# Transposes ahead of their copies, single first blocks on two queues, and short products at unit starts, in one layer of a hybrid decoder

## The chip, the cores and the metric

The kernel runs on one core of one Trainium2 chip. The metric is the device time of one execution in microseconds (us), and the figure to predict is the median over runs. Engines are named as the profile names them: PE is the matrix engine, PEld its weight load, DVE the vector engine, ACT the scalar engine, POOL the general engine, and SP the engine that issues most transfers. "SPq" and "ACTq" are the issue queues of SP and ACT.

## The reference, cut to what matters

One layer works on `x` of 256 tokens by 1024 channels, in float32.

```
h    = RMSNorm(x)
proj = h @ w_in                    # 1024 x 5656: queries, keys, values, gates, merge logits
o_a  = nsa_attention(...)          # compressed, selected and window attention, 8 heads
o_b  = dilated_attention(...)      # 3 groups of 4 heads
mixed = sigmoid(g_a) * (o_a @ w_proj_nsa) + sigmoid(g_b) * (o_b @ w_proj_dil)
x    = x + mixed @ w_out           # 1024 x 1024
h    = RMSNorm(x)
u, gate = split(h @ w_up)          # 1024 x 5632
x    = x + (gelu(conv(u)) * gate) @ w_down     # conv: causal, per channel, width 3; 2816 x 1024
out  = RMSNorm_final(x)
```

## The kernel before

**Work in units.** The host cuts all weights into units of at most 128 x 2240 numbers, in the order of their use, and the loop at the end of the program runs over them. Units 0 to 2 are the first columns of `w_in`; 3 to 15 are its queries, keys and values with the two hidden layers of the compression; 16 to 23 the merge logits; 24 to 26 the two mixer projections (unit 24 is the first half of `w_proj_nsa`); 27 to 30 `w_out`. Unit 31 (`NFIRST`) is the first unit of the feed-forward part: there follow pairs of up units (the `u` half and the gate half of 256 of the 2816 channels), and from the third pair on a down unit behind each pair. A down unit works on what a pair two pairs earlier gave (`LAG = 2`). There are eleven pairs and eleven down units; the last two downs are taken up in a closing part (`last`) of another order.

**One product in three.** All numbers are float32. Each operand is split into a rounded high part and the low rest, and a product is high x high, high x low and low x high. For a weight unit SP loads `raw`, ACT copies it into the high part `whi` (L128, called in `hi_of`, two units ahead), and DVE subtracts that into the low part `wlo` (L132, `lo_of`, one unit ahead). `raw`, `whi` and `wlo` have three buffers each. `parts` then issues on PE first all products with the high weight (L175), then all with the low weight (L180), which need DVE's part. A full unit has 48 products of 256 columns, 32 at L175 and 16 at L180, each with a weight load of its own.

**The short product.** When `rt["kick"]` is set, `parts` issues at its start one product more, of 64 columns (L170), with the operands of the unit's first product. It writes into the first 64 columns of the unit's own accumulator, which the product behind it starts afresh. Before, it is set for one unit, 33 (the third up unit).

**Accumulators.** There are eight banks: tags `d`, `o` and `t` with two tiles of one bank each, and `s` with one tile of two banks. Up pairs alternate between `d` and `o`. The down units add into four banks (`s` and both `t`) over all eleven of them.

**The residual.** The sum `x` after the mixers is held with channels on partitions, as `xT`. The down sums have tokens on partitions, so after unit 32 sixteen transposes (L1150) bring `xT` into four banks and ACT copies each bank into `X` (L1151). These lines are

```
ps2 = pd([2, 512], "s")
for q in range(4):
    t, h = q // 2, q % 2
    p = pd([512], "t") if t == 0 else ps2[:, h]
    for c in range(4):
        T.transpose(p[:, c * 128:c * 128 + 128], xT[:, 4 * h + c, t * 128:(t + 1) * 128], ident)
    A.activation(X[:, t, h * 512:(h + 1) * 512], p, AF.Copy)
```

**The start.** `x` and the weights of units 0 and 1 come together, in five blocks `first` over the eight k tiles of 128 channels (`CHUNKS` says how many k tiles each has). The first block goes out in two halves of 64 partitions, one from SP and one from ACT; all others, then unit 2, `xn`, `small` and the later units go out from SP (`load_to` keeps five units ahead). For each block ACT and DVE split `x` (`split_x`, L199 and L200) and the two weights (L1054 and L1055). Two products of 512 columns on a constant (L1027; the profile shows each as two) run ahead of the first block.

The order on each engine is the order of the code; no scheduler moves anything.

Of the kernel before, what the change touches and what calls it, by code (L numbers as in the profile page):

```python
# [14 lines left out]
AF = mybir.ActivationFunctionType  # L15
# [6 lines left out]
NF = DFF // 256  # L22
DIN = 5656
LAG = 2
CHUNKS = (1, 1, 2, 2, 2)
SHARED = {25: 1024, 26: 1024}
EPS = 1e-6
BIG = 1e30
# [47 lines left out]
def first_units(w):  # L76
# [3 lines left out]
    k0, out = 0, []  # L80
    for n in CHUNKS:
        c = f[:, k0:k0 + n].reshape(128, -1)
# [11 lines left out]
def build(ctx, tc, a, out):  # L94
    nc = tc.nc
    V, A, P, T = nc.vector, nc.scalar, nc.gpsimd, nc.tensor
# [7 lines left out]
    def pd(shape, tag="d"):  # L104
        return ps.tile([128] + shape, F32, name="ps_" + tag, tag=tag, bufs=1 if tag == "s" else 2)

    xT = const.tile([128, 8, S], F32, name="xT")
# [3 lines left out]
    ident = const.tile([128, 128], F32, name="ident")  # L111
# [5 lines left out]
    nhalf, inv_d, epsc = cst[:, 0:2], cst[:, 2:3], cst[:, 3:4]  # L117
# [44 lines left out]
    def parts(groups, w_stationary=True, start=True, stop=True):  # L162


        banks = set()
        if rt.pop("kick", False):

            (wh, _, xh, _), po = groups[0][2][0], groups[0][1]
            l, r = (wh, xh) if w_stationary else (xh, wh)
            T.matmul(po[:, :64], l, r[:, :64], start=True, stop=True, skip_group_check=True)  # L170
        for (bank, po, ks) in groups:
            for (wh, wl, xh, xl) in ks:
                for x in (xh, xl):
                    l, r = (wh, x) if w_stationary else (x, wh)
                    T.matmul(po, l, r, start=start and bank not in banks, stop=False, skip_group_check=True)  # L175
                    banks.add(bank)
        for (bank, po, ks) in groups:
            for n, (wh, wl, xh, xl) in enumerate(ks):
                l, r = (wl, xh) if w_stationary else (xh, wl)
                T.matmul(po, l, r, start=False, stop=stop and n == len(ks) - 1, skip_group_check=True)  # L180

    def w3(u, k):
        n = u.n // k
        return (u.hi[:, u.o:u.o + u.n].rearrange("p (k c) -> p k c", k=k),
                u.lo[:, u.o:u.o + u.n].rearrange("p (k c) -> p k c", k=k))
# [40 lines left out]
    def bc(R, n):  # L226
# [14 lines left out]
    scB = att.tile([128, 16], F32, name="scB")  # L241

    first = [att.tile([128, n * 768 + 8 * (t == "QS")], F32, name="first", tag=t)
             for n, t in zip(CHUNKS, ("QS", "MA", "qb", "kb", "vb"))]
    M = {}

    def mixer_tiles():
# [7 lines left out]
    rt = {}  # L255
# [74 lines left out]
    def mm_first(u):  # L330
# [15 lines left out]
        k0, late = 0, None  # L346
        for n in CHUNKS:
            for v in range(2):
# [264 lines left out]
    def mm_down_part(u, j, tcs, c0=0, c1=512, own=None):  # L613
        wh, wl = w3(u, 2)
        h, l = ffn["a", j]
        parts([((t, ch), ffn["y"][t][ch][:, b:e] if own is None else own,
                [(wh[:, kt, ch * 512 + b:ch * 512 + e], wl[:, kt, ch * 512 + b:ch * 512 + e],
                  h[:, kt, t * 128:t * 128 + 128], l[:, kt, t * 128:t * 128 + 128]) for kt in range(2)])
               for (t, ch) in tcs for b, e in ([(0, 256), (256, 512)] if c1 - c0 == 512 else [(c0, c1)])],
              False, start=j == (0 if own is None else NF - 2), stop=j == NF - 1)  # L620

    def mm_down(j):
        def f(u):
            if j == 0:
                s2 = pd([2, 512], "s")
                ta = pd([512], "t")
                tb = pd([512], "t")
                ffn["y"] = [[s2[:, 0], s2[:, 1]], [ta, tb]]
            if j < NF - 2:
                mm_down_part(u, j, [(t, ch) for t in range(2) for ch in range(2)])  # L630
        return f

# [13 lines left out]
    NFIRST = len(units)  # L646
# [7 lines left out]
    off = -2 * 128 * 2048  # L654
# [344 lines left out]
    u0, u1 = units[0], units[1]  # L999
# [9 lines left out]
    k0 = off = 0  # L1009
    for n, f in zip(CHUNKS, first):  # L1010
        w = f.shape[-1]
        for q, lo, hi in ((nc.sync, 0, 128),) if k0 else ((nc.sync, 0, 64), (nc.scalar, 64, 128)):
            q.dma_start(f[lo:hi], bass.AP(tensor=a["first"].tensor, offset=a["first"].offset + off + lo * w,
                                          ap=[[w, hi - lo], [1, w]]))
        k0 += n
        off += 128 * w
    u2 = units[2]
# [5 lines left out]
    nc.sync.dma_start(sm_, a["small"])  # L1023
    A.activation(tiny[:, 15:16], epsc, AF.Exp)
    pw = pd([512], "t")
    for _ in range(2):
        T.matmul(pw, epsc.to_broadcast([128, 128]), epsc.to_broadcast([128, 512]), start=True, stop=True)  # L1027
    kc0 = att.tile([128, 32], F32, name="kc0")
    V.memset(kc0, 0.0)
    cmp_["kc"] = kc0  # L1030
# [13 lines left out]
    k0 = 0  # L1044
    for n in CHUNKS:
        f = tiles.pop(0)
        f = f[:, 0:n * 768].rearrange("p (k c) -> p k c", k=n)
        for kt in range(k0, k0 + n):
            split_x(kt, f[:, kt - k0, 0:256], first[0][:, 768:776])
        for v, u in enumerate((u0, u1)):  # L1050
            r = f[:, :, 256 + 256 * v:512 + 256 * v]
            h, h32, l = [q[:, k0 * 256:(k0 + n) * 256].rearrange("p (k c) -> p k c", c=256)
                         for q in (u.hi, u.hi.bitcast(F32), u.lo)]
            A.activation(h, r, AF.Copy)  # L1054
            V.tensor_sub(l, r, h32)  # L1055
        k0 += n

# [17 lines left out]
    def at(i):  # L1075
        return items.get(i, [])

    post = []
    for i, u in enumerate(units):
        load_to(i + LA)  # L1080
        for it in at(i - 3):
            it.fin()
        for it in at(i - 2):
            it.te()
        for it in at(i - 1):
            it.sm()
        if i == 10:
            cmp_gelu()
        if i == 2:
            hi_of(3)  # L1090
            lo_of(3)
        if i == 9:
            for it in at(i - 1):
                it.sm2()
        if i > 2:
            lo_of(i + 1)
        if i != 9:
            for it in at(i - 1):
                it.sm2()
        if i == 14:  # L1100
            nc.sync.dma_start(xT, a["xT"])
        if i == 3:
            hi_of(5)
            mixer_tiles()
            u1.evac(u1)
            xc_tile()
            split_cmp(0)
            split_cmp(1)
        if i == 5:
            q_parts(0)  # L1110
            gates_of()
        if i == 6:
            q_parts(1)
        if i == 9:
            cmp_sum()
        if i == 11:
            cmp_kv_ev()
        if i == 14:

            ob = att.tile([128, 4, S], F32R, name="ob", tag="qa")  # L1120
            OB.update(h=ob[:, 0:2], l=ob[:, 2:4])
        if i in (23, 24):
            m = ML[i - 23]
            A.activation(m, m, AF.Sigmoid)
        if i == NFIRST:
            st.close()
            ffn["pool"] = ctx.enter_context(tc.tile_pool(name="ffn", bufs=1))
            gf = ffn["pool"].tile([128, D], F32, name="gf")
            nc.scalar.dma_start(gf, bass.AP(tensor=a["g_final"].tensor, offset=a["g_final"].offset,
                                            ap=[[0, 128], [1, D]]))  # L1130
            X = ffn["pool"].tile([128, 2, D], F32, name="X")
            sq = ffn["pool"].tile([128, 512], F32, name="sq")
        if 24 <= i <= 25:
            hi_of(i + 2)
        if i == NFIRST + 2:
            rt["kick"] = True
        u.mm(u)
        if not 24 <= i <= 26 and i > 1 and i != 3:
            hi_of(i + 2)
        if i == 2:  # L1140
            u0.evac(u0)
        if i == NFIRST + 1:
            rt["R2"] = rows_of(rt["rs2"], "R2", "o")
            units[NFIRST].evac(units[NFIRST])
            ps2 = pd([2, 512], "s")
            for q in range(4):
                t, h = q // 2, q % 2
                p = pd([512], "t") if t == 0 else ps2[:, h]
                for c in range(4):
                    T.transpose(p[:, c * 128:c * 128 + 128], xT[:, 4 * h + c, t * 128:(t + 1) * 128], ident)  # L1150
                A.activation(X[:, t, h * 512:(h + 1) * 512], p, AF.Copy)  # L1151
        if post:
            post.pop()()
        if u.pre:
            u.pre(u)
        if u.evac and i not in (0, 1, NFIRST):
            u.evac(u)
        if u.pre:
            post.append(post_g(len([q for q in units[:i] if q.pre])))
        for it in at(i - 2):  # L1160
            it.pv()
        for it in at(i - 1):
            it.tr()
        for it in at(i):
            it.qk()
        if i == 9:
            cmp_fold()
        if i == 10:
            cmp_kv()
# [63 lines left out]
```

## Time and profile before

| | |
|---|---|
| median of 3 runs | 415.38 us (415.17 to 415.42) |
| the profiled execution, its own time | 412.21 us |
| its span | 410.4 us |
| PE busy | 395.7 us, 96% of the span |
| PEld busy | 384.2 us, 94% |
| DVE busy | 290.6 us, 71% |
| ACT busy | 212.3 us, 52% |
| granted clock of PE, mean over the span | 0.997 |
| read from memory | 71.02 MB, 176 GB/s over the span |

The span runs from the first to the last recorded instruction; the execution's own time has in addition what lies around it. Busy shares are over the whole span, while products on PE overlap one another, so a busy PE is not yet a PE at its quickest. Starts and lengths in rows are us from the start of the span.

### The profile page before, as it was taken

To read this page: it belongs to the slowest core of one execution; us is meant where nothing else is said; L and a number is where in the kernel's file an instruction comes from. 1 tells how busy PE (TensorE), PEld (TensorE's weight loads), DVE (VectorE), ACT (ScalarE), POOL (GpSimd) and SP (SyncE) were. 2 spreads that over 40 slices of the span, in tenths; PEclk is the share of its full clock that TensorE was granted. 3 is DMA by queue.
4 is the path that set the end of the run, shared out by engine and by line. 5 is a ranking of instruction groups with operands and counts; after the bars stand their busy time and mean duration, and the time that the engine had idled before them with its cause. 6 is when DMAs were issued, how large, how long until landed. Compare 5 with 4: busy or idle time off the path is not lost.

```text
span 410.4 us, 8001 instructions
## 1 busy us (share of the span) xinstructions
PE 395.7 (96%) x3409; PEld 384.2 (94%) x3409; DVE 290.6 (71%) x483; ACT 212.3 (52%) x292; POOL 30.7 (7%) x58
## 2 busy tenths in 40 slices
PE   6999999999999999999999799999999999999993
PEld 3999989999998989999999799999999999999992
DVE  3988987887786657468797399494584865946753
ACT  4868563456664345663554766264254552653512
POOL 7010000000000000061143000000000000000012
PEclk9999999999999999999999999999999999999998
DMA  8963755235422532452556336743835627347002
GB/s 272 422 251 119 286 212 206 104 117 232 166 104 102 193 118 104 137 178 101 216 191 238 122 118 232 266 149 160 303 107 207 216 105 296 131 177 277 33 0 102
DMA packets 10851, 72.57 MB, mean 177 GB/s; under 512 B 1216, under 2 KB 1472, under 8 KB 2752
## 3 DMA queue, kind: packets, MB, share of 16 engines
q1 hardware_dynamic: 10448, 71.15, 47.4%
q10 hardware_dynamic: 368, 0.92, 0.7%
q8 instruction: 26, 0.43, 0.4%
q14 instruction: 9, 0.07, 0.1%
HBM read 71.02 MB, written 1.05 MB: 176 GB/s over the span
## 4 chain that ended last, share of the span: by engine, by line
PE 82%; DVE 6%; DMA 6%; ACT 3%; issue 2%; SPq 0%; POOLq 0%; POOL 0%; ACTq 0%
PE ps_d L175 24%; PE ps_o L175 12%; PE ps_d L180 12%; PE ps_o L180 6%; PE ps_s L175 5%; DMA raw<-in_wts_dram 5%; PE ps_t L175 5%; PE ps_d L278 3%; PE ps_s L180 3%; PE ps_t L180 2%; DVE wlo L132 2%; PE ps_o L892 1%; PE ps_s L933 1%; PE ps_o L540 1%; PE ps_t L879 1%
## 5 line engine op out<-in xcount | busy, mean ns | idle before, releaser
L132 DVE TENSOR_TENSOR wlo<-raw,whi 128x2048 fp32r<-128x2048 f32 (+2 forms) x61 | 135.2, 2218 | 2.7 <-ACT whi L128 2.7
L128 ACT ACTIVATE whi<-raw 128x2048 fp32r<-128x2048 f32 (+1 forms) x61 | 114.8, 1883 | 34.2 <-DMA raw<-in_wts_dram 30.2
L175 PE MATMUL ps_d<-hTh,whi 128*128 128x256 f32 x384 | 90.3, 281 | 0.4 <-DVE qb L448 0.4
L175 PE MATMUL ps_d<-hTl,whi 128*128 128x256 f32 x384 | 89.2, 278 | 0.0
L175 PEld LDWEIGHTS ps_d<-hTh,whi 128*128 128x128 f32 x384 | 72.3, 188 | 2.2 <-issue 1.9
L175 PEld LDWEIGHTS ps_d<-hTl,whi 128*128 128x128 f32 x384 | 72.3, 188 | 0.0
L180 PE MATMUL ps_d<-hTh,wlo 128*128 128x256 f32 x384 | 47.9, 278 | 0.0
L180 PEld LDWEIGHTS ps_d<-hTh,wlo 128*128 128x128 f32 x384 | 45.7, 188 | 0.0
L175 PE MATMUL ps_o<-hTh,whi 128*128 128x256 f32 x160 | 36.9, 277 | 0.0
L175 PE MATMUL ps_o<-hTl,whi 128*128 128x256 f32 x160 | 36.8, 276 | 0.0
L579 ACT ACTIVATE C<-U,small 128x256 f32<-128x256 f32 x22 | 12.0, 594 | 46.3 <-DVE U L575 46.3
L175 PEld LDWEIGHTS ps_o<-hTl,whi 128*128 128x128 f32 x160 | 30.1, 188 | 0.0
L175 PEld LDWEIGHTS ps_o<-hTh,whi 128*128 128x128 f32 x160 | 30.1, 188 | 0.0
L583 DVE SCALAR_TENSOR_TENSOR C<-U,small,C 128x256 f32<-128x256 f32 x44 | 19.4, 482 | 7.5 <-ACT C L579 7.4
L175 PE MATMUL ps_s<-whi,al 128*128 128x256 f32 x88 | 21.3, 281 | 0.0
L175 PE MATMUL ps_s<-whi,ah 128*128 128x256 f32 x88 | 21.3, 281 | 0.0
L856 ACT ACTIVATE E<-E,ast 128x256 f32<-128x256 f32 (+1 forms) x32 | 14.2, 444 | 13.1 <-DVE ast L851 13.1
L575 DVE TENSOR_TENSOR U<-ps_d,R 128x512 f32<-128x512 f32 x6 | 4.1, 691 | 23.1 <-PE ps_d L180 19.2
L175 PE MATMUL ps_t<-whi,ah 128*128 128x256 f32 x84 | 20.4, 282 | 0.0
L175 PE MATMUL ps_t<-whi,al 128*128 128x256 f32 x84 | 20.4, 281 | 0.0
L180 PE MATMUL ps_o<-hTh,wlo 128*128 128x256 f32 x160 | 19.8, 276 | 0.0
L132 POOL TENSOR_TENSOR wlo<-raw,whi 128x1024 fp32r<-128x1024 f32 x3 | 7.8, 2594 | 155.9 <-ACT whi L128 155.9
(266 smaller groups left out, 763.3 us busy)
## 6 DMA issues: line engine op xcount, KB each, us to landing
raw<-in_wts_dram SPq DMA_DIRECT2D x61, 1024.0 KB, 4.8
first<-in_first_dram SPq DMA_DIRECT2D x3, 768.0 KB, 8.5
raw<-in_wts_dram SPq DMA_DIRECT2D x1, 1120.0 KB, 12.0
xn<-in_xn_dram SPq DMA_DIRECT2D x2, 512.0 KB, 12.8
xT<-in_xT_dram SPq DMA_DIRECT2D x1, 1024.0 KB, 6.8
gf<-in_g_final_dram ACTq DMA_DIRECT2D x1, 512.0 KB, 3.5
out_dram<-X SPq DMA_DIRECT2D x1, 512.0 KB, 2.6
first<-in_first_dram SPq DMA_DIRECT2D x1, 384.0 KB, 4.4
```

Source lines behind the costliest of these rows:

```text
L128: A.activation(u.hi[:, u.o + c0:u.o + c1], u.raw[:, c0:c1], AF.Copy)
L132: (eng or V).tensor_sub(u.lo[:, u.o + c0:u.o + c1], u.raw[:, c0:c1], u.hi.bitcast(F32)[:, u.o + c0:u.o + c1])
L175: T.matmul(po, l, r, start=start and bank not in banks, stop=False, skip_group_check=True)
L180: T.matmul(po, l, r, start=False, stop=stop and n == len(ks) - 1, skip_group_check=True)
L278: T.matmul(u.p[:, i], l[:, kt, i * 128:i * 128 + 128], r[:, kt], start=kt == 0 and i == 0 and q == 0, stop=kt == 7 and q == 2, skip_group_ ...
L540: T.matmul(u.p[:, i], l[:, kt, i * 128:i * 128 + 128], r[kt // 4][:, kt % 4], start=kt == 0 and i == 0 and q == 0, stop=kt == 7 and q == 2 ...
L579: A.activation(C[:, c], U[:, c, 2:], AF.Identity, scale=CW(2, t), bias=CB[:, t:t + 1])
L583: V.scalar_tensor_tensor(C[:, c], U[:, c, w:w + S], CW(w, t), C[:, c], op0=OP.mult, op1=OP.add)
L856: A.activation(self.E[:, i], self.E[:, i], AF.Exp, bias=mn[:, i:i + 1], scale=-1.0, accum_out=dn[:, i:i + 1])
L879: T.transpose(p[:, i], self.E[:, 4 * c + 2 * g + b, k * 128:(k + 1) * 128], ident)
L892: T.matmul(oA[js[c]][g * 64:g * 64 + 64, t * 128:(t + 1) * 128], Vn[:, k, b * 128 + g * 64:b * 128 + g * 64 + 64], self.PT[:, i], start=t ...
L933: T.matmul(self.ps[c][:, q], M["qb"][h:h + 64, i, t * 128:(t + 1) * 128], M["kb"][h:h + 64, i, :nk], start=True, stop=True)
```

## The change

Five edits, all to the order or the number of instructions; the results are the same numbers.

1. All sixteen residual transposes come first and then the four copies.
2. `CHUNKS` becomes `(1, 1, 1, 1, 2, 2)`: six first blocks. Each goes out whole; the second from ACT, the other five from SP.
3. The high part of the first k tile of unit 0 is copied by DVE in place of ACT.
4. The products on a constant ahead of the first block become three, of 512, 512 and 256 columns.
5. `kick` now takes a value. With `"own"` the short product goes into the unit's own accumulator, for units 24 and 33. With a tag it goes into a tile of 64 columns of that tag, which nothing reads; this is set for each of the first nine down units, `"o"` and `"d"` in turn.

```
-CHUNKS = (1, 1, 2, 2, 2)
+CHUNKS = (1, 1, 1, 1, 2, 2)
...
-        if rt.pop("kick", False):
+        kick = rt.pop("kick", None)
+        if kick:
             (wh, _, xh, _), po = groups[0][2][0], groups[0][1]
             l, r = (wh, xh) if w_stationary else (xh, wh)
-            T.matmul(po[:, :64], l, r[:, :64], start=True, stop=True, skip_group_check=True)
+            po = pd([64], kick) if len(kick) == 1 else po[:, :64]
+            T.matmul(po, l, r[:, :64], start=True, stop=True, skip_group_check=True)
...
             if j < NF - 2:
+                rt["kick"] = "od"[j % 2]
                 mm_down_part(u, j, [(t, ch) for t in range(2) for ch in range(2)])
...
-        for q, lo, hi in ((nc.sync, 0, 128),) if k0 else ((nc.sync, 0, 64), (nc.scalar, 64, 128)):
-            q.dma_start(f[lo:hi], bass.AP(tensor=a["first"].tensor, offset=a["first"].offset + off + lo * w,
-                                          ap=[[w, hi - lo], [1, w]]))
+        (nc.scalar if k0 == 1 else nc.sync).dma_start(f, bass.AP(tensor=a["first"].tensor, offset=a["first"].offset + off,
+                                                                 ap=[[w, 128], [1, w]]))
...
-    for _ in range(2):
-        T.matmul(pw, epsc.to_broadcast([128, 128]), epsc.to_broadcast([128, 512]), start=True, stop=True)
+    for n in (512, 512, 256):
+        T.matmul(pw[:, :n], epsc.to_broadcast([128, 128]), epsc.to_broadcast([128, n]), start=True, stop=True)
...
+        if k0 == 0:
+            V.tensor_copy(u0.hi[:, 0:256], f[:, 0, 256:512])
...
-            A.activation(h, r, AF.Copy)
+            if k0 or v:
+                A.activation(h, r, AF.Copy)
...
-        if i == NFIRST + 2:
-            rt["kick"] = True
+        if i in (24, NFIRST + 2):
+            rt["kick"] = "own"
...
+            pt = [pd([512], "t"), pd([512], "t"), ps2[:, 0], ps2[:, 1]]
             for q in range(4):
-                t, h = q // 2, q % 2
-                p = pd([512], "t") if t == 0 else ps2[:, h]
                 for c in range(4):
-                    T.transpose(p[:, c * 128:c * 128 + 128], xT[:, 4 * h + c, t * 128:(t + 1) * 128], ident)
-                A.activation(X[:, t, h * 512:(h + 1) * 512], p, AF.Copy)
+                    T.transpose(pt[q][:, c * 128:c * 128 + 128], xT[:, 4 * (q % 2) + c, q // 2 * 128:q // 2 * 128 + 128],
+                                ident)
+            for q in range(4):
+                A.activation(X[:, q // 2, q % 2 * 512:q % 2 * 512 + 512], pt[q], AF.Copy)
```

The rows below are the program's own order on an engine, with the semaphores that an instruction waits for in brackets. Line numbers after the change are higher by two at L170 to L220, and by four at the transposes.

PE at the residual transposes, before, from the rows of `R` (L220) to the start of unit 33:

```order
L220 MATMUL ps_o<-ident,tiny 128x128 [waits PE_49,Pool_49]
L220 MATMUL ps_o<-ident,tiny 128x128
L1150 MATMUL ps_t<-ident,xT 128x128 [waits DMAHW2_49]
L1150 MATMUL ps_t<-ident,xT 128x128 x7
L1150 MATMUL ps_s<-ident,xT 128x128 x4
L1150 MATMUL ps_s<-ident,xT 128x128 [waits Activation_49]
L1150 MATMUL ps_s<-ident,xT 128x128 x3
L170 MATMUL ps_o<-hTh,whi 128x64 [waits PE_49]
```

The same place on PE after the change:

```order
L222 MATMUL ps_o<-ident,tiny 128x128 [waits PE_49,Pool_49]
L222 MATMUL ps_o<-ident,tiny 128x128
L1154 MATMUL ps_t<-ident,xT 128x128 [waits DMAHW2_49]
L1154 MATMUL ps_t<-ident,xT 128x128 x7
L1154 MATMUL ps_s<-ident,xT 128x128 x8
L172 MATMUL ps_o<-hTh,whi 128x64 [waits Activation_49]
L177 MATMUL ps_o<-hTh,whi 128x256
L177 MATMUL ps_o<-hTl,whi 128x256
```

The wait for ACT in the middle of the transposes is gone, and the short product of unit 33 now waits for an instruction of ACT (L214, the copy out of the bank of `mean_sq`, L212 before) where it waited for one of PE.

PE at the second down unit, before, from the low products of the up unit ahead of it:

```order
L180 MATMUL ps_o<-hTh,wlo 128x256 [waits DVE_49]
L180 MATMUL ps_o<-hTh,wlo 128x256 x15
L175 MATMUL ps_s<-whi,ah 128x256 [waits Activation_49]
L175 MATMUL ps_s<-whi,al 128x256
L175 MATMUL ps_s<-whi,ah 128x256
```

The same place after the change:

```order
L182 MATMUL ps_o<-hTh,wlo 128x256 [waits DVE_49]
L182 MATMUL ps_o<-hTh,wlo 128x256 x15
L172 MATMUL ps_d<-whi,ah 128x64 [waits Activation_49]
L177 MATMUL ps_s<-whi,ah 128x256
L177 MATMUL ps_s<-whi,al 128x256
```

One product of 64 columns has come in, into a tile of the tag that the next pair of up units uses, and it carries the wait that the first product of the unit carried.

SP at the start of the program, before (ACT issues one more transfer of 64 x 776):

```order
L1013 DMA first<-in_first_dram 64x776
L1013 DMA first<-in_first_dram 128x768
L1013 DMA first<-in_first_dram 128x1536 x3
L155 DMA raw<-in_wts_dram 128x2240
L1022 DMA xn<-in_xn_dram 128x1024 x2
```

The same place after the change (ACT issues one more transfer of 128 x 768, the second block):

```order
L1015 DMA first<-in_first_dram 128x776
L1015 DMA first<-in_first_dram 128x768 x2
L1015 DMA first<-in_first_dram 128x1536 x2
L155 DMA raw<-in_wts_dram 128x2240
L1024 DMA xn<-in_xn_dram 128x1024 x2
```

SP issues five first blocks as before; the block from ACT is a whole one of 128 partitions where it was a half one, and the load of unit 2 stands behind the same number of transfers.

## Rows read from the trace of the kernel before

**Rows 1.** The page: its first line, and the chain that ended last, by engine.

```profile
span 410.4 us, 8001 instructions
...
PE 82%; DVE 6%; DMA 6%; ACT 3%; issue 2%; SPq 0%; POOLq 0%; POOL 0%; ACTq 0%
```

**Rows 2.** PE's waits: total us, how often, the longest.

```profile
PE ps_d L342 <- ACT whi L1054: 3.2, 3, 2.0
PE ps_s L1150 <- ACT X L1151: 2.5, 1, 2.5
...
PE ps_o L732 <- DVE S L725: 0.7, 1, 0.7
PE ps_d L175 <- DVE qb L448: 0.4, 1, 0.4
```

**Rows 3.** Timeline, 224 to 233 us: start, busy us, instruction, [idle before and what ended it].

```profile
224.36 0.26 ACT L212 ACTIVATE tiny<-ps_o,cst 128x2 f32<-128x2 f32 x1 [2.26 <-PE ps_o L207]
...
227.53 1.04 PE L1150 MATMUL ps_t<-ident,xT 128*128 128x128 f32 x8
...
228.41 0.60 PE L1150 MATMUL ps_s<-ident,xT 128*128 128x128 f32 x4
228.88 1.09 ACT L579 ACTIVATE C<-U,small 128x256 f32<-128x256 f32 x2 [0.76 <-DVE U L575]
...
231.47 0.66 PE L1150 MATMUL ps_s<-ident,xT 128*128 128x128 f32 x4 [2.46 <-ACT X L1151]
231.86 0.19 PEld L170 LDWEIGHTS ps_o<-hTh,whi 128*128 128x128 f32 x1
...
231.97 0.19 PEld L175 LDWEIGHTS ps_o<-hTh,whi 128*128 128x128 f32 x1
...
232.17 0.60 ACT L1151 ACTIVATE X<-ps_s 128x512 f32<-128x512 f32 x1 [0.75 <-PE ps_s L1150]
```

**Rows 4.** Timeline of DVE, 234 to 245 us.

```profile
234.74 0.69 DVE L591 TENSOR_TENSOR C<-C,R 128x512 f32<-128x512 f32 x1 [3.47 <-ACT C L590]
...
236.15 2.28 DVE L132 TENSOR_TENSOR wlo<-raw,whi 128x2048 fp32r<-128x2048 f32 x1
...
242.00 2.28 DVE L132 TENSOR_TENSOR wlo<-raw,whi 128x2048 fp32r<-128x2048 f32 x1
```

**Rows 5.** Chain in order of time, 65 to 256 us: start, us, what.

```profile
65.63 1.81 PE ps_d L180 x16
...
173.07 1.88 PE ps_d L180 x16
...
209.88 3.77 PE ps_o L175 x32
...
237.70 3.63 PE ps_o L175 x32
241.33 1.81 PE ps_o L180 x16
...
246.77 1.81 PE ps_d L180 x16
...
254.02 1.88 PE ps_s L175 x16
```

**Rows 6.** Chain in order of time, 0 to 61 us: the weight loads in it.

```profile
5.92 14.85 DMA raw<-in_wts_dram
...
42.22 4.73 DMA raw<-in_wts_dram
```

**Rows 7.** Timeline of DVE at two of the four units of `w_out`.

```profile
204.26 0.69 DVE L549 TENSOR_TENSOR xT<-xT,ps_o 128x512 f32<-128x512 f32 x1 [0.70 <-PE ps_o L180]
...
209.91 0.69 DVE L549 TENSOR_TENSOR xT<-xT,ps_o 128x512 f32<-128x512 f32 x1
```

**Rows 8.** Timeline, 0 to 10 us: SP's issues of first blocks, ACT's third block.

```profile
0.72 2.62 SPq L1013 DMA_DIRECT2D first<-in_first_dram  x5
...
9.04 0.91 ACT L199 ACTIVATE hTh<-first 128x256 fp32r<-128x256 f32 x2 [1.98 <-DMA first<-in_first_dram]
```

More of the change, by code (lines that the diff above doesn't have):

```diff
@@ L243, in build @@
     first = [att.tile([128, n * 768 + 8 * (t == "QS")], F32, name="first", tag=t)
-             for n, t in zip(CHUNKS, ("QS", "MA", "qb", "kb", "vb"))]
+             for n, t in zip(CHUNKS, ("QS", "MA", "qb", "MB", "kb", "vb"))]
     M = {}
```

## The prediction

> **What bounds the kernel now.** I read the page first. The span is 410.4 us and the chain that ended last is 82% matrix engine, 6% DVE, 6% DMA, 3% ACT [rows 1]: over most of the program an instruction more or less on PE is time, and only where another engine or a transfer ends a wait does PE's work cost nothing. The profiled execution took 412.21 us, 1.8 more than its span, and the median of the three runs is 415.38, 3.2 above it. I make the sum in differences against the profiled execution and put it on the median, as if what lies between the two stayed as it is.
>
> Next the list of PE's waits, longest first [rows 2]. There are four that matter: 3.2 us in three pieces for the first weight copies (L1054), 2.5 us once for a residual copy (L1151), 0.7 and 0.4 us for DVE around 45 and 60 us. After the last of these, PE waits for one thing in 340 us, the residual copy. Then the timeline around that wait [rows 3], the chain for the pace of the products [rows 5], and the chain of the first 64 us [rows 6].
>
> **Part 1, the transposes.** Sixteen transposes move `xT` into `X`. The first twelve run from 227.53 on at 0.11 us each (eight from 227.53 to 228.41) [rows 3]. The last four write the second bank of the tile `ps_s`, whose first bank the third copy reads, and they start at 231.47, behind that copy, after 2.46 us of idle PE. The copy is late because ACT does the two `C` products and two copies first. In the changed order no transpose stands behind a copy: the four start at 228.41 + 4 x 0.11 = 228.85, **2.62 us earlier**, and the unit behind them too. Its short product now waits for an ACT instruction (order of the change, front section); the bank it writes was last read by ACT at 224.36 (L212) [rows 3], so that wait is long over.
>
> What is late next? PE moves by 2.62, ACT only by the 0.75 us that its fourth copy waited [rows 3], and DVE, which waits for ACT's gelu (3.47 us), by the same 0.75 [rows 4]. So unit 34's low part, done at 236.15 + 2.28 = 238.43 now, is done at 237.68, and PE wants it at 241.33 - 2.62 = 238.71: 1.0 us to spare. Unit 35's is done at 244.28 - 0.75 = 243.53 and wanted at 246.77 - 2.62 = 244.15: 0.6 to spare [rows 4, 5]. Later ones have more. The bound from below is that this cover fails by the difference, so that 1 of the 2.62 us is lost; I take all 2.62.
>
> **Part 2, the nine short products before the down units.** Each is one more weight load and a 64-column product, with its own accumulator bank, so nothing new waits: it takes over the waits of the product behind it. Cost: the existing short product's weight load starts at 231.86 and the next at 231.97, so 0.11 us for a product of a quarter the columns; the loads are the limit [rows 3]. Nine make 1.0 us. The Trainium skill (TensorE: Matmul & The Clock Gate, "Back-to-back issue gap") gives products of up to 64 columns a gap of about 60 cycles, an estimate of 25 ns each here. By it the nine would cost 0.23 us and the time would come out 0.8 us lower; the row with the weight load in it decides against that.
>
> What they may bring is pace. Identical streams of 256-column products run at two paces in this trace: 3.63 us for 32 (113 ns) in up units, 3.77 for 32 (118 ns) in all output units, 1.88 for 16 (117.5 ns) in every down unit [rows 5]. Pace is kept while nothing intervenes: between 178 and 222 us seven units and more stay slow. It is chosen where the stream is interrupted. Of the 14 projection units from 61 to 175 us, nearly all behind short attention products, 8 have 1.81 or 1.82 us in their last 16 products and 6 have 1.88 or 1.89 (first and last shown) [rows 5]. The one short product of this kind, at 231.88, ends a slow stretch, and the unit behind it is quick. The down units now are always entered from a 256-column product and always slow; up units are entered from them and always quick. So the price of a down unit has two ends: quick, 48 x (117.5 - 113.4) = 0.20 us gained and 0.11 paid, nine times **-0.8 us**; slow as now, nine times **+1.0 us**. I take the first, because the two kinds of row nearest to it, the existing short product and the mixed entries (8 of 14), lean that way, but only a little.
>
> **Part 3, the short product before the first mixer projection.** If it turns the slow stretch from there on quick, seven units of 48 products at 4.1 ns make 1.4 us on PE. But DVE is as tight in it: for the output units its add (L549) stands at 204.26 after 0.70 us of waiting for PE, and at 209.91 with no wait, 5.65 apart, PE's own slow pace [rows 7]. A quicker PE would wait for DVE, so at most about 0.7 us comes through. If it stays slow it costs 0.11. This unit comes already behind short products (the attention's) and is slow, so I take **+0.1**, with -0.7 as the other end.
>
> **Part 4, the start.** The first blocks go out as six loads of 1, 1, 1, 1, 2, 2 k tiles for five, the first whole on SP, the second on ACT; DVE takes one of the first copies; the warm-up gets half a product more. ACT idles 1.98 us before the third block at 9.04 [rows 8], and single k tiles should land earlier there. This brings little: PE's first wait of 3.2 us is not the chain. The chain to 61 us runs through the third weight load after these blocks, which lands at 5.92 + 14.85 = 20.77, then ACT, then DVE, and later one more load at 42.22 [rows 6]. PE waits 0.4 and 0.7 us for that chain [rows 2], and whatever PE gains before 20 us ends in those waits; what it loses up to 1.1 us they cover too, if the chain itself stands. Only that load's landing counts. The bytes ahead of it are the same and SP issues five blocks as before, in 2.62 us, 0.52 each [rows 8]. So I take 0, with one such issue time to either side: -0.5 to +0.5. The added warm-up and DVE copy lie beside the first blocks, in time that those two waits cover. The Trainium skill (DMA: Bandwidth & Descriptors, "Issuing engines are not separate DMA queues") says that transfers started from several engines share the same 16 DMA engines and only issue time is saved, which speaks against a gain here.
>
> **Sum.** -2.62 - 0.8 + 0.1 + 0 = -3.3 us: the profiled execution at 408.9, the median at **412.1**.
>
> **Rivals.**
> 1. *The down units stay slow.* For: all of them are now, and six of 14 other entries are. The sum is -2.62 + 1.0 + 0.1 = -1.5: 413.9 us. With the mixer stretch quick 413.1.
> 2. *The gain of part 1 is given back.* PE comes 2.62 us earlier to low parts that move by 0.75. If copies, table load and gelu follow more slowly than I add them, 1 us or more goes into new waits at units 34 and 35; with slow down units that is 414.9, with quick ones 413.1. Against: 1.0 and 0.6 us to spare.
> 3. *Slower: the pace of the up units is lost.* Up units are quick because of how they are entered from a down unit. If the short products change that and 18 of them run at 118 ns, each pair costs 96 x 4.1 ns = 0.39 us, nine pairs 3.5; with 1.1 for the short products and -2.62 that is +2.0: 417.4. It turns the sign when the 1.5 us that rival 1 leaves is used up, at four pairs. Against: the up unit's own entry, from the same kind of down product, is not touched.
> 4. *The start moves.* The load at 20.77 lands 0.5 us later or earlier: any of these cases, moved by 0.5.
>
> **How the numbers follow.** The main case 0.50, rival 1 0.33, rival 2 with more than 1 us lost 0.08, rival 3 0.05, others 0.04. The main case alone spans 411.0 (mixer stretch quick, load a little earlier) to 412.6; rival 1 spans 413.0 to 414.4. The range, 410.9 to 414.2, holds nearly all of the first and most of the second. Below 0.2% (0.83 us, about what a measurement of this kernel can tell from no change) either way counts as same: part 1 alone is three times that. Faster 0.90, same 0.05, slower 0.05.
>
> **What would show it.** After: no wait of `ps_s` transposes on `X`; transposes of 0.11 us each without a break and the next unit near 229.3; 16 products in 1.81 us in down units if they are quick, in 1.88 if not; nine 64-column products 0.11 us apart from what follows; the third weight load's landing near 20.8; PE's waits near 45 and 60 us still there. The prediction is wrong if PE waits for DVE at units 34 to 36, if the down or up units run slow, or if the landing at 20.8 moves by more than 0.5.

## The result

The changed kernel takes 411.14 us (median of 4, 410.94 to 412.53) against 415.40 before (415.38 when the forecast was made, with one run fewer): ratio 0.9904, 95% interval 0.9881 to 0.9927. The forecast was 412.1. The gain of 4.3 us is larger than the sum forecast, and the sum is made up otherwise: two of its terms had the wrong sign, and a cost that was in no term went away with one of the waits.

The profiled execution of the changed kernel took 411.17 us, near its median. Its page (span; granted clock in 40 slices, tenths; the chain by engine), against [rows 1]:

```profile
span 409.4 us, 8037 instructions
...
PEclk9999899999999999999999999999999999999997
...
PE 75%; DVE 14%; DMA 5%; ACT 3%; issue 2%; POOLq 0%; SPq 0%; POOL 0%; ACTq 0%; DVEq 0%
```

The same slices of the clock in the kernel before:

```profile
PEclk9999999999999999999999999999999999999998
```

The span fell by 1.0 us only, while the median fell by 4.3. And the fifth slice, 41 to 51 us, has an 8 in the clock, where it had a 9 before. Both are taken up below. DVE has grown in the chain from 6% to 14%.

PE's waits in the changed kernel (total us, times, longest), against [rows 2]:

```profile
PE ps_d L177 <- DVE qb L450: 1.8, 1, 1.8
...
PE ps_d L182 <- DVE wlo L132: 0.8, 1, 0.8
PE ps_o L735 <- DVE S L728: 0.7, 1, 0.7
PE ps_d L280 <- DVE wlo L132: 0.5, 1, 0.5
```

The 2.5 us for the residual copy are gone, and so are the 3.2 us for the first weight copies. The wait for `qb` near 45 us has grown from 0.4 to 1.8.

Timeline of the changed kernel (start, busy us, instruction), against [rows 3, 4, 8]: the first loads, the two output adds and the place of the transposes.

```profile
0.72 2.36 SPq L1015 DMA_DIRECT2D first<-in_first_dram  x5
...
9.18 0.91 ACT L201 ACTIVATE hTh<-first 128x256 fp32r<-128x256 f32 x2 [0.49 <-DMA first<-in_first_dram]
...
204.92 0.67 DVE L551 TENSOR_TENSOR xT<-xT,ps_o 128x512 f32<-128x512 f32 x1
...
210.56 0.67 DVE L551 TENSOR_TENSOR xT<-xT,ps_o 128x512 f32<-128x512 f32 x1
...
228.16 1.04 PE L1154 MATMUL ps_t<-ident,xT 128*128 128x128 f32 x8
...
229.03 1.04 PE L1154 MATMUL ps_s<-ident,xT 128*128 128x128 f32 x8
...
229.82 0.28 PE L172 MATMUL ps_o<-hTh,whi 128*128 128x64 f32 x1
...
231.45 1.08 ACT L1157 ACTIVATE X<-ps_s 128x512 f32<-128x512 f32 x2
...
235.91 2.28 DVE L132 TENSOR_TENSOR wlo<-raw,whi 128x2048 fp32r<-128x2048 f32 x1
```

The sixteen transposes now run without a break from 228.16 to 229.82, and unit 33 begins there; the copies from `ps_s` come 1.6 us behind it and hold up nobody. The two adds (L551) are 5.64 us apart with no wait ahead of either: DVE sets the pace of the `w_out` units now, where one of the two waited 0.70 us for PE before [rows 7].

Chain of the changed kernel in order of time (start, us, what), against [rows 5, 6]:

```profile
5.91 14.94 DMA raw<-in_wts_dram
...
45.40 5.53 PE ps_d L177 x32
...
177.29 0.23 PE ps_d L172
177.52 1.91 PE ps_d L177 x16
...
180.34 1.81 PE ps_d L177 x16
...
239.27 1.81 PE ps_o L182 x16
...
251.96 0.03 PE ps_o L172
252.00 1.96 PE ps_s L177 x16
253.96 1.89 PE ps_t L177 x16
...
257.73 3.65 PE ps_o L177 x32
```

Three things stand there. The projections behind the new short product at 177.29 run at 1.81 us for 16: quick. The down unit behind the one at 251.96 runs at 1.89 for 16: slow, as before. And the 32 products at 45.40 took 5.53 us in place of 3.63 to 3.77. The windows of the changed kernel around the last (us, PE busy and instructions, granted clock, share of the transfer engines, GB/s) say why:

```profile
43.60:45.40 1.80, 0.00 (x0) 1.00 0.84 332
45.40:46.90 1.50, 1.50 (x13) 0.99 0.68 284
46.90:50.30 3.40, 3.40 (x18) 0.50 0.54 161
50.30:60.00 9.70, 9.70 (x81) 1.00 0.73 269
```

PE is idle for 1.8 us, goes on at the full clock for 1.5 us, and then has the lower of its two levels (1.2 of 2.4 GHz) for 3.4 us. In its trace 16 products start in this stretch, 213 ns apart, where some 29 would at the full clock's 118 ns; the x18 counts also products that only reach into it.

### The profile page after: what moved, and what is told of

It reads as the page before. It is cut to its first block, busy times and chain, and to the rows that moved or that the text cites. A ratio compares the mean times of both kernels' runs of the same rounds, so it can differ in the third digit from the quotient of the medians.

```text
span 409.4 us, 8037 instructions
## 1 busy us (share of the span) xinstructions
PE 397.6 (97%) x3421; PEld 386.2 (94%) x3421; DVE 291.1 (71%) x486; ACT 212.2 (52%) x293; POOL 31.2 (8%) x58
## 4 chain that ended last, share of the span: by engine, by line
PE 75%; DVE 14%; DMA 5%; ACT 3%; issue 2%; POOLq 0%; SPq 0%; POOL 0%; ACTq 0%; DVEq 0%
PE ps_d L177 24%; PE ps_d L182 12%; PE ps_o L177 9%; DVE wlo L132 5%; PE ps_s L177 5%; PE ps_t L177 5%; PE ps_o L182 5%; DMA raw<-in_wts_dram 4%; PE ps_s L182 3%; PE ps_t L182 2%; DVE hTl L202 2%; PE ps_o L895 2%; PE ps_s L936 1%; PE ps_d L280 1%; PE ps_t L882 1%
## 5 line engine op out<-in xcount | busy, mean ns | idle before, releaser
L177 PE MATMUL ps_d<-hTh,whi 128*128 128x256 f32 x384 | 91.7, 283 | 1.8 <-DVE qb L450 1.8
L177 PE MATMUL ps_d<-hTl,whi 128*128 128x256 f32 x384 | 90.6, 281 | 0.0
L177 PEld LDWEIGHTS ps_d<-hTh,whi 128*128 128x128 f32 x384 | 73.4, 191 | 3.6 <-issue 3.3
L177 PEld LDWEIGHTS ps_d<-hTl,whi 128*128 128x128 f32 x384 | 73.4, 191 | 0.0
```

## The experiments

Two theories were on record before the runs. **A:** the timed executions of the kernel before hold stretches at the lower clock behind PE's idle times, one of them behind the residual copy, that its one profiled execution lacked; so the transposes are worth their wait and such a stretch. **B:** the stretch stands at the wait for `qb` in both kernels, and the start has to bring what the sum lacks. A rival to the cause within A is **C:** the low clock comes whatever PE does in those gaps. Ratios are to the kernel before on the same chip in the same session (414.17 us in the first four runs, 414.80 in the next four, 414.81 in the last four).

**The kernel before, once more.** No edit.

> The kernel before, unchanged, to see an execution of the common length: the profiled one took 412.2 us, the timed ones 415.4. Theory A (the timed executions have a stretch at the lower clock behind PE's 2.46 us of idle at the residual copy, which the profiled one lacked): a profile near 415.4 us, mean clock about 0.985 to 0.99 in place of 0.997, the low clock from 231 us on, some 3 us long in added time. Theory B (the low clock stands behind the wait for qb near 45 us, as in the changed kernel): the same mean clock, but the low stretch at 46 to 52 us. If neither holds, a profile again near 412.2.

414.56 us (412.85 to 416.75), ratio 1.0018, 0.9994 to 1.0042. Its profiled execution took 414.70 us. Its windows, same columns:

```profile
8.50:10.50 2.00, 0.00 (x0) 1.00 1.00 412
10.50:11.80 1.30, 1.29 (x10) 0.99 1.08 456
11.80:15.20 3.40, 3.40 (x18) 0.50 0.98 377
15.20:229.70 214.50, 213.82 (x1872) 1.00 0.49 177
229.70:232.20 2.50, 0.04 (x2) 1.00 0.23 95
232.20:233.60 1.40, 1.40 (x12) 1.00 0.00 0
233.60:237.00 3.40, 3.40 (x19) 0.51 0.00 0
```

Two low stretches, each behind an idle of 2.0 to 2.5 us and 1.3 to 1.4 us of work: one behind the wait for the third first block, which neither theory had placed, and one behind the residual copy, where A had. Its span is 412.8, 2.4 us over that of the first profile [rows 1]: most of the 3.2 us that the first profile lacked against its own median. In this execution nothing happens at 46 us, against B.

**The transposes alone.** On the kernel before, edit 1 of the change:

```
+            pt = [pd([512], "t"), pd([512], "t"), ps2[:, 0], ps2[:, 1]]
             for q in range(4):
...
+            for q in range(4):
+                A.activation(X[:, q // 2, q % 2 * 512:q % 2 * 512 + 512], pt[q], AF.Copy)
```

> Only the transposes ahead of the copies, on the kernel before. Theory A: PE's idle is gone, 2.6 us, and the low clock behind it, about 3 us: 409.6 to 410.2 us, mean clock 0.997. Theory B: the idle alone, 2.6 us: 412.8, with the low clock near 46 us still there. The step of the prediction was 2.62 us.

409.73 us (409.62 to 410.57), ratio 0.9908, 0.9878 to 0.9939: A's number, 4.4 us off the median, where the idle alone is 2.6. Its profile has no low clock between 10 us and the last product.

**The start alone.** On the kernel before, edits 2 to 4:

```
+CHUNKS = (1, 1, 1, 1, 2, 2)
...
+        (nc.scalar if k0 == 1 else nc.sync).dma_start(f, bass.AP(tensor=a["first"].tensor, offset=a["first"].offset + off,
+                                                                 ap=[[w, 128], [1, w]]))
...
+    for n in (512, 512, 256):
...
+            V.tensor_copy(u0.hi[:, 0:256], f[:, 0, 256:512])
```

> Only the start of the change on the kernel before (six first blocks, the second from ACT, one copy on DVE, longer warm-up). Theory A: PE comes 2.4 us earlier to a wait for DVE that ends no earlier, idles longer at 45 us and falls to the lower clock, as in the profile of the changed kernel: 1.5 us more, 416.9. Theory B: no such loss against the timed executions before, and what is missing in the sum of the others, 1.6 us, is gained: 413.8. The step of the prediction was 0 within 0.5.

414.92 us (413.6 to 415.94), ratio 1.0023, 1.0002 to 1.0044: a little slower, between the forecast of 0 and A's 1.5. PE's waits in it:

```profile
PE ps_s L1154 <- ACT X L1155: 2.5, 1, 2.5
PE ps_d L177 <- DVE qb L450: 1.8, 1, 1.8
```

The 3.2 us of waits at the start are gone, and 1.8 us have come at `qb`. Its windows behind the two idle times:

```profile
45.10:51.00 5.90, 5.87 (x51) 1.00 0.64 237
...
231.50:235.00 3.50, 3.50 (x19) 0.51 0.00 0
```

In this profile the low clock stood behind the residual copy, not behind `qb`, though PE idled there for the same 1.8 us as in the changed kernel: a given gap leads to it in some executions only.

**The change without the short products at the down units.** On the changed kernel:

```
             if j < NF - 2:
-                rt["kick"] = "od"[j % 2]
```

> The changed kernel without the nine short products ahead of the down units. Its profile shows these units at 118 ns for a product as before, and the nine short products at 0.11 us each. By the profile 0.93 us less than the changed kernel, 410.2 us. By the prediction's main case (the down units quick with the short product) 0.8 us more: 411.9.

408.57 us (408.46 to 409.94), ratio 0.9887, 0.9855 to 0.9919. Three of its five executions took 408.5 and two 409.9; the profiled one was of the latter, with the low clock at 46.6 us.

**The changed kernel, once more.** No edit.

> The changed kernel, unchanged, on the chip and beside the runs on which its parts are compared. If the nine short products cost 0.11 us each as its profile shows, 0.9 to 1.0 us above the version without them (408.57): 409.5. If their cost is hidden or they bring pace somewhere, at or below 408.6. As first timed, 411.14, if the two sessions differ by nothing.

410.57 us (409.71 to 413.11), ratio 0.9900, 0.9870 to 0.9930. That the nine short products cost something is likely by this, but the two ranges overlap; the later pair settles it.

**Transposes and the short product of unit 24, no more.** On the kernel before, edit 1 and

```
-        if i == NFIRST + 2:
+        if i in (24, NFIRST + 2):
```

> The kernel before with the transposes first and the short product before the first mixer projection, and nothing else. By the changed kernel's profile the projections and output units then run at 113 ns and 0.9 us comes through, DVE limiting the rest: 408.8 against 409.73 for the transposes alone. By the prediction's term (this unit stays slow) 0.1 us more, 409.8. Beside the version with the start in addition (408.57) it gives the price of the start: about 0 if 408.6, a loss by the start if lower, a gain if higher.

409.37 us (408.40 to 410.37), ratio 0.9866, 0.9839 to 0.9893. It has the old start, and its profile the low clock from 11.6 to 15.0 us. It is not to be told from the run without the product by time alone; the profiles do that: from unit 24 to unit 33 52.63 us here, 53.57 without it.

**Work in the idle time at the residual copy.** On the kernel before, where PE waits:

```
+            dm = pd([512], "o")
             for q in range(4):
...
+                if q == 3:
+                    for _ in range(21):
+                        T.transpose(dm[:, 0:128], xT[:, 0, 0:128], ident)
```

> The kernel before, with 21 transposes of one block more, into a bank that nothing reads, while PE waits for the residual copy; they are extra work, and the wait itself stays. Theory A (what PE's idle costs is the 2.5 us itself and, in most executions, a stretch of 3.4 us at the lower clock behind it, 1.5 us): no low clock behind 230 us, and 1.0 to 1.5 us less than before, 412.9. Theory C (the low clock comes whatever PE does there): the low clock is still seen, and no gain, 414.2.

413.19 us (412.45 to 414.71), ratio 0.9966, 0.9949 to 0.9984. More work in less time, though the wait itself stayed: unit 24 to unit 33 took 56.25 us in its profile, 56.16 without the filling. Its windows:

```profile
43.50:45.40 1.90, 0.11 (x2) 1.00 0.93 345
...
46.30:49.70 3.40, 3.40 (x18) 0.50 0.39 84
...
230.60:232.90 2.30, 2.27 (x21) 1.00 0.09 36
232.90:240.00 7.10, 6.96 (x59) 1.00 0.01 2
```

Behind the filled gap the clock stays at 1.00. By itself this does not put C out, since the first profile of the kernel before kept its clock behind the unfilled gap too; the next run does more. In this execution the third first block came early (ACT took it up at 7.51 us, at 9.04 in [rows 8]), PE idled before `qb` as the changed kernel does, and the low clock came there: B's place, in one of the six profiles that have the old start. The gain is 1.6 us by the medians and 1.4 by the ratio, and the profile holds a cost beside it, which its chain shows:

```profile
233.73 3.85 PE ps_o L175 x32
...
239.47 3.77 PE ps_o L175 x32
```

Units 33 to 36, quick in [rows 5], ran slow here, 0.8 us in all, with nothing changed but what PE did ahead of them.

**Work in the idle time at `qb`.** On the changed kernel without the down products:

```
+        if i == 7:
+            dm = pd([512], "o")
+            for _ in range(15):
+                T.transpose(dm[:, 0:128], ident, ident)
```

> The changed kernel without the nine short products, and with 15 transposes of the identity, into a bank that nothing reads, while PE waits for DVE near 44 us. Theory A: the fall to the lower clock at 46.6 us, in two of three profiles with this wait, is gone; up to 1.5 us less in the executions that had it, and about 408.4 for all, with less spread than 408.5 to 409.9. Theory C: the fall stays, the time too, 408.6.

408.73 us (408.58 to 408.88), ratio 0.9849, 0.9825 to 0.9873. Its windows:

```profile
43.40:45.20 1.80, 1.68 (x16) 1.00 0.92 332
...
46.60:50.00 3.40, 3.40 (x33) 1.00 0.46 147
```

33 instructions in the 3.4 us that held 18 in the changed kernel. The median is that of the run without the filling; the executions of 409.9 are gone. This run and the next three all have the `qb` wait filled, and none of their four profiles has the low clock there; of the five profiles with 1.8 us of idle PE at that place four have it. C is out.

**One short product at each down unit, on that kernel.** The line `rt["kick"] = "od"[j % 2]` put back.

> The kernel of the filled qb wait (408.73, hardly any spread) with the one short product ahead of each of nine down units put back. PE from unit 33 to its end took 171.53 us without and 172.55 with them in the profiles: 409.75. If a down unit ran quick with it, 407.9.

409.66 us (409.28 to 409.73), ratio 0.9879, 0.9853 to 0.9906: 0.93 us more, with ranges far apart. The two were timed in different sessions, on different chips, on which the kernel before took 414.81 and 414.80; their ratios to it overlap. The profiles, 1.02 us apart from unit 33 on, say the same. A loss.

**Two short products at each down unit.** The same, and in `parts`

```
+            for _ in range(2 if len(kick) == 1 else 1):
+                T.matmul(po, l, r[:, :64], start=True, stop=True, skip_group_check=True)
```

> The same with two short products ahead of each of the nine down units, since the quick unit 33 is entered through a product 112 ns ahead of it, and the down unit through one 27 ns ahead. If the second gives that entry, the units run at 113 ns: 2 x 1.02 paid, 9 x 48 x 4.5 ns = 1.9 gained, 408.8. If the pace of a down unit does not hang on its entry: 2.0 above 408.73, 410.8.

410.73 us (410.54 to 411.17), ratio 0.9910, 0.9880 to 0.9939. The time is that of "slow", but the chain shows another thing:

```profile
250.08 0.14 PE ps_o L173 x2
250.22 1.91 PE ps_s L178 x16
252.12 1.81 PE ps_t L178 x16
...
255.75 3.77 PE ps_o L178 x32
...
267.06 0.14 PE ps_d L173 x2
267.20 1.96 PE ps_s L178 x16
269.17 1.88 PE ps_t L178 x16
...
272.94 3.65 PE ps_d L178 x32
```

The first down unit is quick (1.81), the up pair behind it slow (3.77), the second down unit slow again, the next pair quick; the first, third, fifth, seventh and ninth down units are quick, the others slow. What the down units win the up units lose. The quick down units are also the ones whose short products go to `o`, the slow ones those with `d`; this run does not part the two.

**No short product before the first mixer projection.** On the kernel of the filled `qb` wait, `if i in (24, NFIRST + 2)` back to `if i == NFIRST + 2`.

> The kernel of the filled qb wait without the short product before the first mixer projection. By the profiles (52.62 us from the first mixer product to unit 33 with it, 53.57 without) 0.95 us more than 408.73: 409.7. By the prediction's term for it, 0.1 less: 408.6.

409.37 us (409.26 to 409.71), ratio 0.9875, 0.9849 to 0.9902: 0.64 us more than with it, again across the two sessions. Its chain has, where the changed kernel has 1.81:

```profile
178.65 1.88 PE ps_d L177 x16
```

From unit 24 to unit 33 its profile took 53.51 us, and 52.62 with the product. So this product does bring the quick pace, and pays.

**The old start with its idle filled.** On the kernel with transposes first and the product of unit 24:

```
+            if k0 == 2:
+                dm = pd([512], "o")
+                for _ in range(16):
+                    T.transpose(dm[:, 0:128], ident, ident)
```

> The old start with transposes first and the mixer product (409.37, 408.4 to 410.4, low clock at 11.6 us in its profile), and 16 transposes of the identity, into a bank that nothing reads, in PE's idle before the third first block near 8.5 us. Theory A: the low clock at 11.6 us is gone, and its 1.5 us where it stood; 408.4 to 408.8, which prices the changed start at 0 within 0.3. Theory C: 409.4 as without the filling.

409.06 us (408.90 to 409.83), ratio 0.9869, 0.9842 to 0.9896. No low clock in its profile between the first 9 us and PE's last product; 0.3 us below the kernel without the filling, with overlapping ranges and in another session.

## Why the prediction was right, and where it was not

The stages of PE's own timeline in the profiled executions, in us (from the first product of unit 24 to the short product of unit 33, and from there to PE's last end), put each term beside its size:

| kernel | to unit 24 | 24 to 33 | 33 to the end | clock below full in between |
|---|---|---|---|---|
| before, first profile | 175.69 | 56.19 | 171.52 | none |
| before, once more | 176.42 | 56.16 | 173.17 | at 11.8 and 233.6 |
| transposes alone | 175.66 | 53.57 | 171.53 | none |
| changed | 177.22 | 52.60 | 172.55 | at 46.9 |
| changed, no down products | 176.99 | 52.62 | 171.53 | at 46.6 |
| that, `qb` wait filled | 175.62 | 52.62 | 171.53 | none |
| that, no product at unit 24 | 175.56 | 53.51 | 171.53 | none |
| old start, its wait filled | 175.96 | 52.78 | 171.53 | none |

In the prediction's own terms the case that came is rival 1 with the mixer stretch quick, 413.1, and by the sign that it named for being wrong, down units that run slow, its main case did not come. That 412.1 lies 1.0 us from the measured 411.14 is in part luck: part 2 was 1.8 us too hopeful, and part 3 with the low clock behind the residual copy gave some 2.5 us beyond the sum.

**Part 1 was right**: 56.19 - 53.57 = 2.62. That it fits to the hundredth is luck, since other profiles of the same two stages (56.16 and 56.31 with the wait, 53.51 without) put it between 2.6 and 2.8. What it would make late did not come: unit 34's low part ended at 235.91 + 2.28 = 238.19, and its products with it began at 239.27 in the chain, 1.1 us later, where 1.0 was forecast. Rival 2 is out.

**What failed first is the ground of the sum**, "as if what lies between the two stayed as it is". Of the 3.2 us between the profiled execution and the median, the 2.4 that the second profile shows are low clock behind PE's idle times. The part of it behind the residual copy, 173.17 - 171.52 = 1.65 us, went with the wait. The forecast of that wait's worth was 2.6; the run gave 4.4.

**Part 2: the step that failed is "I take the first", the quick end.** The down units stayed slow, rival 1 in its mechanism, and the nine short products cost 172.55 - 171.53 = 1.02 us in the profiles and 0.93 in the timed pair, the +1.0 that stood there as the other end, not the -0.8 of the sum. The price of one was right: 0.11 us. By the Trainium skill (TensorE: Matmul & The Clock Gate, "Back-to-back issue gap") the nine would have cost 0.23, an estimate. The chain shows both, 0.03 us to the next product's start, as the page has the gap, and then 1.96 in place of 1.88 behind it [rows 5]. In the timeline its weight load starts at 251.69 and the next at 251.81, the step of all the loads around it, so each short product takes one more place in the row of loads.

**Part 3 failed the other way.** "I take +0.1" should have been a gain: the units from 24 on turned quick, and 0.9 us came through in the profiles (53.51 - 52.62), 0.64 in the timed pair. The bound by DVE was right in kind, as the adds without a wait show, and its size, 0.7, lies between the two.

**Part 4 was right on the load that it followed, and lacked a mechanism.** The third weight load landed at 5.91 + 14.94 = 20.85, where it landed at 20.77 before; what PE gained ahead of 20 us ended in the wait for `qb` (0.4 us before, at 45 us; the 0.7 of the prediction's pair stands at 61). What was not seen is that a longer wait there can bring the lower clock: it did in both profiles of the changed kernel, and 16 products at 213 in place of 118 ns are 1.5 us. The old start has the like behind its own gap at 8.5 us, where the later waits cover a part (176.42 against 175.69, 0.7 us). Alone the start measured 1.0023, a loss at the edge of what can be told; beside the other edits 408.57 stands against 409.37, and with both gaps filled 408.73 against 409.06, which lean the other way. Both of these pairs were timed in different sessions, and by the ratios the first turns round (0.9887 against 0.9866). The profiles that have no low clock up to unit 24 agree with the second: the new start reaches unit 24 at 175.33 to 175.62 us in five of them, the old at 175.66 to 175.96 in three, some 0.3 us later. So the new start gains about that where the low clock does not come, and the low clock at `qb` costs 1.4 to 1.6 (176.99 and 177.22 against 175.62). Its price in the changed kernel stays open between these.

The account against the second profile of before: 177.22 - 176.42 = +0.8 at the start, 52.60 - 56.16 = -3.6 for transposes and unit 24, 172.55 - 173.17 = -0.6 for the low clock gone and the down products come; in sum -3.4, as the spans, 409.4 and 412.8. The executions that set the median of before are about 0.7 us longer than that one.

Rival 3, up units that lose their pace, did not come with one product, but it did with two. Why the pace turns where it does is not settled. The runs show that it changes at entries, between up and down units too, and is kept within a unit: behind a slow down unit the up pair was quick in all these chains, behind a quick one slow; behind a quick up pair the down unit was slow with no product or one ahead of it, and quick with two; behind a slow up pair it was slow with none and with two. In the run with two, the bank of the short products (`o` or `d`) alternates in step with this, so that it may be the bank and not the pair ahead; no run tells them apart.

The best version is the changed kernel without the nine products and with the `qb` wait filled: 408.73, ratio 0.9849, and executions within 0.3 us of one another, where those of the kernel before lie between 411.0 and 417.7.

## What to carry to other kernels

Where a profiled execution is quicker than the median, here by 0.8%, the difference belongs in the working: it may be a cost of the very wait that is to be removed, and a second profile of the same kernel shows it. An idle time of PE between dense stretches can cost more than its length, and work that nobody needs can be worth putting into it. A product added to change PE's pace has to be judged by the units behind those that it is meant for as well.

## What the hardware showed that was not expected

The granted clock fell to half for 3.4 us (16 products 213 ns apart for some 29 at 113 to 118) behind PE idle times of 1.8, 2.0 and 2.5 us, not at once but 0.3 to 1.5 us after PE had gone on. The same gap led to it in some executions and not in others: in four of five profiles with the 1.8 us, in two of three each with the 2.0 and the 2.5. A stretch cost 1.5 to 1.65 us behind the residual copy, where nothing covered it. Transposes that nobody reads, run in the gap, kept the clock up behind it in each of the six profiles that had them.

Identical 256-column products have two paces, 113 and 118 ns, each kept over a unit and often over several. Which of them holds changed with what ran ahead of a unit: with one product of 64 columns in one place (unit 24), with two but not one in another (every second down unit), and with 21 transposes more ahead of unit 33.
